# Two mixture-of-experts layers: slots of the fixed experts listed ahead of the ranking, weights queued in order of use, three blocks added by one-hot products

## The chip, the cores and the metric

The kernel is one program on 1 core of one Trainium2 chip. The metric is the device time of one execution in microseconds (us), lower is better. Before the change it was 2995.12 us, the median of 3 runs (2994.06 to 2997.8).

## What is computed

A block of 512 tokens of width 1024 (with 256 context tokens in the first layer) goes through two layers, a mixer and then a mixture of experts each, and after them through a second network (feed-forward, a mixer, feed-forward, a gate). The change is in the mixture of experts, which runs twice: for 768 tokens (layer 0) and for 512 (layer 1).

```python
def hier_moe(h, ...):                      # 4 groups of 8 experts, each 1024 -> 512 -> 1024
    g_idx = argmax(h @ grp_w + grp_b)      # one group for each token
    top_v, top_i = top_k(logits of the 8 experts of that group, 2)
    w = g_prob * softmax(top_v)
    return routed_experts(h, e_idx, w, ...)
# each token's two experts e:  y += w_e * ((silu(x @ w_gate[e]) * (x @ w_up[e])) @ w_down[e])
x = x + g2 * hier_moe(h2)
```

All 32 experts of a layer are computed, and the weights of one are 6.3 MB of float32.

## The kernel before

**Blocks.** `moe` (L830) works by blocks of 128 rows. The experts are ranked by the number of their tokens; experts 0 and 1 are always put first (`FIRST`), so that their weights can be loaded before the routing is known. These two and the next 8 ranked ones (4 in layer 1, `MANY`) have a block each. The rest go in pairs, 64 rows for each of two experts, whose products run side by side in two halves of TensorE's columns. That makes 2 + 8 + 11 = 21 blocks in layer 0 and 2 + 4 + 13 = 19 in layer 1. `turn` (L930) is their order: the two fixed ones, then single and pair in turn, then the pairs that are left. Tokens beyond a block's rows go through a loop that starts at block 12 (`overflow`).

**Routing.** `router` (L601) finds each token's two experts (`oh`), its position among the tokens of that expert (`pos`, L658) and the weights (`v3`). `places` (L664) ranks the experts and gives each choice its block (`ohb`) and its slot. `slots` (L724) turns that into lists by one-hot products: for each block the tokens, the rows and the weights (`stok`, `srow`, `swt`). `order_list` (L700) gives the experts in order of rank, which SyncE reads (L720) to address the weights. `token_major` (L897) writes the normed tokens as rows to DRAM (`h2d`), in 256 KB pieces issued by SyncE (L912).

**Blocks in time.** Block e gathers its rows with an indirect DMA from POOL (L942, tile `xg`), transposes them (L1073), then multiplies by gate, up (L1089) and down (L1108). The down product is scaled (L1115) and scattered to `Yd` in DRAM (L951). Each weight tile is 512 KB; a single block needs 12, a pair 24. They are all issued by SyncE (`raw`, L117, L131), into a ring of 24 tiles: 5 that other stages use too, 13 that exist only here, and 6 that are the split buffers of other stages. A tile's slot is free when the tile 24 places before it has been multiplied. The program's order is gate of block e, down of e-1, up of e.

**End of the stage.** The rows of the last block are not scattered; zeros are written in their place before the first block. After the last down product SyncE reads `Yd` back (L991, 1 MB for each 128 tokens), and the weights of the next stage wait behind these reads. The last block's rows are added to X by products with a one-hot matrix `own` (L1005 to L1012). Then for each 128 tokens the two rows of a token are added on POOL (L1020), transposed (L1030, L1028), scaled and added to X (L1035, L1040, L1041), squared (L1045, L1048), summed over k on VectorE (L1050) and over partitions by a product with ones (L1051). The sums give the norm of the next stage.

Instructions are placed on each engine's queue by a list scheduler with its own model of times, so the order in the trace is not always the order of the text.

Of the kernel before, what the change touches and what calls it, by code (L numbers as in the profile page):

```python
# [21 lines left out]
KD = 8  # L22
# [37 lines left out]
class Kernel:  # L60
    def __init__(self, tc, A):
        self.tc, self.nc, self.A = tc, tc.nc, A
        self.n = 0
        self.live = []
        self.fenced, self.behind, self.last_raw = 0, [], None
# [51 lines left out]
    def raw(self, src, queue=None):  # L117
# [483 lines left out]
    def router(self, l, lt, pool, p2, n_tok):  # L601
# [58 lines left out]
        V.tensor_copy(cnt, pc[:, :NE])  # L660
        self.choice = (oh, pos, v3, cnt)
        return self.places(l, p2, tt)

    def places(self, l, pool, tt):  # L664

        V = self.nc.vector
        oh, pos, _, cnt = self.choice
        mk = lambda name, *s, dt=F32: pool.tile([128, *s], dt, name="p" + name)
# [19 lines left out]
        n = nb + nb % 2  # L688
        ohb = mk("ohb", tt, 2, n)
        V.tensor_tensor(ohb, self.iota[:, :n].unsqueeze(1).unsqueeze(1).to_broadcast([128, tt, 2, n]),  # L690
# [7 lines left out]
        return ohb, slot, nb  # L698
# [25 lines left out]
    def slots(self, pool, rel, rhs, n_tok, name, bufs):  # L724
# [15 lines left out]
        row = pool.tile([128, n], I32, name=name + "row")  # L740
        V.tensor_copy(row, f)
        tok = pool.tile([128, n], I32, name=name + "tok")
        V.tensor_scalar(tok, row, 1, None, op0=ALU.arith_shift_right)
        wt = pool.tile([128, n], F32, name=name + "wt")
# [32 lines left out]
    def overflow(self, l, n_tok, h2d, Yd, p2, x):  # L777
# [7 lines left out]
        with tc.If(nb > 0):  # L785
            with tc.For_i(0, nb, 1) as i:
                with ExitStack() as st:
# [25 lines left out]
                    row, tok, wt = self.slots(pool, rel, rhs, n_tok, "o", 2)  # L813
# [16 lines left out]
    def moe(self, l, n_tok, fg, side_work, stats):  # L830
# [8 lines left out]
        with ExitStack() as st:  # L839
# [4 lines left out]
            with ExitStack() as st1:  # L844
# [3 lines left out]
                with ExitStack() as st2:  # L848
# [65 lines left out]
                    ohb, slot, nb = self.router(l, lt, pool, p2, n_tok)  # L914
                    v3 = self.choice[2]
                    n = ohb.shape[-1]
                    rhs = p2.tile([128, tt, 2, 3 * n], F32R, name="rhs", tag="lg")
                    for c in range(3):
                        V.tensor_tensor(rhs[:, :, :, n * c:n * c + n], ohb,
                                        v3[:, c].bitcast(F32).unsqueeze(3).to_broadcast([128, tt, 2, n]), ALU.mult)  # L920
# [3 lines left out]
                    srow, stok, swt = [pool.tile([128, n], d, name=x) for x, d in (("srow", I32), ("stok", I32), ("swt", F32))]  # L924
                    for a, b in ((srow, row), (stok, tok), (swt, wt)):
                        V.tensor_copy(a, b)
                    self.order_list(l, pool, p2)

                n1 = FIRST[l] + MANY[l]
                turn = list(range(FIRST[l]))  # L930
                for i in range(nb - n1):
                    turn += [FIRST[l] + i] * (i < MANY[l]) + [n1 + i]
                ranks = lambda b: [b] if b < n1 else [2 * b - n1, 2 * b - n1 + 1]
                ysc = []
                with ExitStack() as st2:
                    p2 = st2.enter_context(tc.tile_pool(name=f"moee{l}", bufs=1, reuse_waits="tile"))
                    xg = [xg0] + [p2.tile([128, D], F32, name=f"xg{i}") for i in (1, 2)]
                    ex = []

                    def start(e):  # L940
                        x, b = xg[e % 3], turn[e]
                        nc.gpsimd.indirect_dma_start(  # L942
                            out=x, out_offset=None, in_=h2d,
                            in_offset=bass.IndirectOffsetOnAxis(ap=stok[:, b:b + 1], axis=0),
                            bounds_check=n_tok - 1, oob_is_err=False)
                        ex.append(self.expert(p2, l, [self.ranked_expert(l, r) for r in ranks(b)], x))
                        next(ex[e])

                    def put(e, y):
                        b = turn[e]  # L950
                        ysc.append(nc.gpsimd.indirect_dma_start(  # L951
                            out=Yd, out_offset=bass.IndirectOffsetOnAxis(ap=srow[:, b:b + 1], axis=0),
# [3 lines left out]

                    start(0)
# [3 lines left out]
                    put(nb - 1, xg[2])  # L961
                    for e in range(nb):
# [7 lines left out]
                        if e:  # L970
                            put(e - 1, self.rows_of(p2, next(ex[e - 1]), swt[:, turn[e - 1]:turn[e - 1] + 1]))
# [4 lines left out]
                        if e == self.pause:  # L976
                            self.overflow(l, n_tok, h2d, Yd, p2, xg[(e + 2) % 3])
# [5 lines left out]
                for _ in side_work:  # L983
                    pass
# [1249 lines left out]
```

## Time and profile before

| | |
|---|---|
| median of the timed runs | 2995.12 us (2994.06 to 2997.8) |
| the profiled execution | 2992.93 us, its span 2991.3 us |
| mean granted TensorE clock | 0.97 |
| PE, DVE, ACT, POOL busy | 93%, 41%, 30%, 15% |
| DMA of the span | 643 MB, mean 215 GB/s |

The profile is of one execution; times in it are from the start of its span. PE is TensorE's multiplying, PEld its loading of weights, DVE VectorE, ACT ScalarE, POOL GpSimd, SPq SyncE's queue. A busy PE is not PE at its peak. A number in brackets in a timeline is the idle time ahead of an instruction and what ended it. Layer 0's expert stage runs from about 395 to 931 us, layer 1's from about 1319 to 1838 us.

### The profile page before, as it was taken

How to read it: one execution, taken by the hardware profiler on the slowest of the kernel's cores; microseconds unless marked ns; L12 is line 12 of the kernel's file. 1: busy time of each engine (PE TensorE's matmuls, PEld its weight loads, DVE VectorE, ACT ScalarE, POOL GpSimd, SP SyncE). 2: the span in 40 equal slices, each digit the busy share in tenths (PEclk: the TensorE clock that was granted, in tenths of full speed). 3: DMA queues.
4: the chain of work that ended last, by engine and by line, in shares of the span. 5: the costliest groups of instructions: out<-in, count | busy, mean ns of one | idle time of the engine just before them, and what ended most of it. 6: DMA issues, size and time to landing. Idle time of an engine off the chain costs nothing.

```text
span 2991.3 us, 34947 instructions
## 1 busy us (share of the span) xinstructions
PE 2770.2 (93%) x12662; PEld 1815.0 (61%) x12662; DVE 1231.7 (41%) x2183; ACT 910.5 (30%) x1488; POOL 451.9 (15%) x430
## 2 busy tenths in 40 slices
PE   7989979998997999979999997999999889999998
PEld 3756734433433889844433333778888767888886
DVE  3883431000005566542000004954436777444335
ACT  3563201110102467511110002333225666323223
POOL 1662110000002000010100001371003140000000
PEclk9999989999998999989999998899999999999999
DMA  7558569999997211448999997343333422333331
GB/s 245 198 191 291 177 203 382 403 404 394 399 403 306 77 52 29 149 162 316 406 412 414 412 414 298 92 131 116 94 97 117 134 64 76 97 94 96 99 92 64
DMA packets 211426, 642.98 MB, mean 215 GB/s; under 512 B 32016, under 2 KB 41328, under 8 KB 209968
## 3 DMA queue, kind: packets, MB, share of 16 engines
q1 hardware_dynamic: 195648, 609.38, 56.2%
q0 software_dynamic: 15600, 31.32, 3.0%
q8 instruction: 101, 1.65, 0.2%
q14 instruction: 77, 0.63, 0.1%
HBM read 624.37 MB, written 37.19 MB: 221 GB/s over the span
## 4 chain that ended last, share of the span: by engine, by line
PE 62%; DMA 22%; DVE 9%; issue 4%; ACT 2%; SPq 1%; POOL 0%; DVEq 0%; POOLq 0%; ACTq 0%
PE ps L167 13%; PE ps L168 13%; PE ps L169 13%; PE ps L1089 9%; DMA raw<-exp_w_up 7%; DMA raw<-exp_w_down 6%; DMA raw<-exp_w_gate 6%; PE ps L1108 5%; PE ps L357 3%; DVE wl L90 1%; PE ps L1073 1%; DMA raw<-w_in_ab 1%; PE ps L219 1%; PE ps L1332 0%; DVE X L1035 0%
## 5 line engine op out<-in xcount | busy, mean ns | idle before, releaser
L1089 PE MATMUL ps<-raw,xt 128*64 128x512 f32 (+1 forms) x2048 | 635.6, 602 | 14.9 <-DMA raw<-exp_w_up 10.9
L167 PE MATMUL ps<-Hh,wh 128*128 128x512 f32 (+1 forms) x1320 | 495.5, 381 | 7.2 <-ACT Hh L260 2.1
L169 PE MATMUL ps<-Hh,wl 128*128 128x512 f32 (+1 forms) x1320 | 495.6, 377 | 6.4 <-DVE wl L90 6.3
L168 PE MATMUL ps<-Hl,wh 128*128 128x512 f32 (+1 forms) x1320 | 496.3, 377 | 1.6 <-DVE Hl L267 1.2
L1089 PEld LDWEIGHTS ps<-raw,xt 128*64 128x64 f32 (+1 forms) x2048 | 213.4, 150 | 389.6 <-issue 271.7
L88 ACT ACTIVATE wh<-raw 128x1024 fp32r<-128x1024 f32 (+1 forms) x224 | 231.5, 1039 | 559.8 <-PE ps L168 455.3
L90 DVE TENSOR_TENSOR wl<-raw,wh 128x1024 fp32r<-128x1024 f32 (+1 forms) x224 | 275.4, 1233 | 186.7 <-ACT wh L88 186.0
L1094 DVE TENSOR_TENSOR eh<-ps,eh 128x512 f32<-128x512 f32 x40 | 27.7, 692 | 753.7 <-PE ps L1089 704.8
L1108 PE MATMUL ps<-raw,ht 128*64 128x512 f32 (+1 forms) x1024 | 327.2, 603 | 2.3 <-issue 1.7
L167 PEld LDWEIGHTS ps<-Hh,wh 128*128 128x128 f32 x1320 | 248.9, 190 | 71.2 <-issue 5.6
L168 PEld LDWEIGHTS ps<-Hl,wh 128*128 128x128 f32 x1320 | 249.9, 189 | 52.5 <-issue 2.5
L169 PEld LDWEIGHTS ps<-Hh,wl 128*128 128x128 f32 x1320 | 249.1, 189 | 53.1 <-DVE wl L90 7.6
L1108 PEld LDWEIGHTS ps<-raw,ht 128*64 128x64 f32 (+1 forms) x1024 | 123.2, 150 | 192.7 <-issue 167.3
L1115 ACT ACTIVATE ey<-ps,swt 128x512 f32<-128x512 f32 x76 | 51.4, 686 | 323.8 <-PE ps L1108 305.3
L951 POOL DMA_INDIRECT yd<-ey,srow x38 | 37.9, 997 | 694.5 <-ACT ey L1115 579.5
L408 POOL TENSOR_TENSOR cg<-cg,cp 128x798 f32<-128x798 f32 x60 | 119.1, 1985 | 107.0 <-DVE cv L415 72.1
L1092 ACT ACTIVATE eh<-ps 128x512 f32<-128x512 f32 x40 | 23.9, 597 | 335.0 <-PE ps L1089 335.0
L1078 ACT ACTIVATE xt<-ps 128x512 f32<-128x512 f32 x40 | 23.9, 597 | 279.2 <-PE ps L1089 150.1
L357 PE MATMUL ps<-raw,sc 128*32 128x512 f32 x384 | 97.8, 614 | 3.5 <-DMA raw<-mod_w 3.5
L167 PE MATMUL ps<-Gh,wh 128*128 128x512 f32 x256 | 101.1, 395 | 0.0
L169 PE MATMUL ps<-Gh,wl 128*128 128x512 f32 x256 | 101.0, 395 | 0.0
L168 PE MATMUL ps<-Gl,wh 128*128 128x512 f32 x256 | 101.0, 395 | 0.0
(698 smaller groups left out, 3938.4 us busy)
## 6 DMA issues: line engine op xcount, KB each, us to landing
raw<-exp_w_up SPq DMA_DIRECT2D x256, 512.0 KB
raw<-exp_w_gate SPq DMA_DIRECT2D x256, 512.0 KB
raw<-exp_w_down SPq DMA_DIRECT2D x256, 512.0 KB
raw<-ffn_w SPq DMA_DIRECT2D x132, 512.0 KB
raw<-mod_w SPq DMA_DIRECT2D x96, 512.0 KB
yr<-yd SPq DMA_DIRECT2D x10, 1024.0 KB
X<-xT SPq DMA_DIRECT2D x16, 384.0 KB
raw<-w_in_ab SPq DMA_DIRECT2D x12, 512.0 KB
```

The costliest lines, as they stand in the source:

```text
L88: self.nc.scalar.activation(dst.hi, src, AF.Copy)
L90: self.split_last = eng.tensor_tensor(dst.lo, src, dst.hi.bitcast(F32), ALU.subtract).ins
L167: mm(ps, a.hi, b.hi, start=start, stop=False)
L168: mm(ps, a.hi, b.lo, start=False, stop=False)
L169: mm(ps, a.lo, b.hi, start=False, stop=stop)
L219: self.sums_last = self.nc.tensor.matmul(ps[:, t:t + 1], s, self.ones, start=True, stop=True).ins
L357: nc.tensor.matmul(ps[32 * g:32 * g + 32], self.sc[:, 2 * g + j, 30 - 2 * i:62 - 2 * i], w[:, j * 512:(j + 1) * 512], start=i == 0 and j = ...
L408: nc.gpsimd.tensor_tensor(a, a, t, ALU.add)
L951: ysc.append(nc.gpsimd.indirect_dma_start(out=Yd, out_offset=bass.IndirectOffsetOnAxis(ap=srow[:, b:b + 1], axis=0), in_=y, in_offset=None ...
L1089: mm(ps[s], XT[:, 2 * c + k, s], w[:, 512 * k:512 * k + 512], start=c == 0 and k == 0, stop=c == 3 and k == 1, **kw)
L1108: mm(pss[b][s], HT[:, k, s], w[:, 512 * b:512 * b + 512], start=k == 0, stop=k == 3, **kw)
L1115: self.nc.scalar.activation(y[:, 512 * b:512 * b + 512], pss[b], AF.Copy, scale=wt)
```

## The change

Four edits in `moe` and its helpers.

1. The lists of the two fixed experts are made by a first call of `slots`, from `oh` and `pos` alone, ahead of `token_major` and of `places`; the lists of all other blocks by a second call behind `places`.
2. `turn` has the pair before the single one, and every weight tile of the stage is put on SyncE's queue behind the one that the program asked for before it (`in_turn`).
3. The last three blocks (`owned`), not one, are added to X by one-hot products (`add_own`).
4. The other rows are read back while the last two blocks run (`add_rows`), in 512 KB reads issued by POOL into the ring of weight tiles; the two rows of a token are added on VectorE. Squares and sums are made for each k behind the last block's `add_own`: the sum over partitions by products with ones or squared gains (`gs`), with no sum over k on VectorE but a small one at the end. The next stage's weights no longer wait for the reads.

```diff
@@ raw
-            if ins:
-                st.enter_context(self.tc.issue_after(ins))
+            for i in (ins, self.in_turn and queue is None and self.last_raw):
+                if i:
+                    st.enter_context(self.tc.issue_after(i))
@@ moe
-                    ohb, slot, nb = self.router(l, lt, pool, p2, n_tok)
...
-                    row, tok, wt = self.slots(p2, slot, rhs, n_tok, "s", 2 * tt)
+                    self.router(l, lt, pool, p2, n_tok)
+                    oh, pos, v3, _ = self.choice
...
+                    first = lists("f", oh[:, :, :, :n0], pos, 4)
                     token_major()
                     self.behind = [None] * self.ahead[l] + put_back[1::2]
+                    later = lists("s", *self.places(l, p2, tt), 4)
                     self.order_list(l, pool, p2)
...
-                    turn += [FIRST[l] + i] * (i < MANY[l]) + [n1 + i]
+                    turn += [n1 + i] + [n0 + i] * (i < MANY[l])
...
+                    def add_own(e, pss):
+                        w = swt(turn[e])
+                        YS = self.split_tile(self.turn_of(self.wrings)[0], [128, CH], "w")
...
+                        for k in range(KD):
+                            for i, (o, c) in enumerate(segs):
+                                ps = self.bank("tp")
+                                for j in (YS.hi, YS.lo):
+                                    nc.tensor.matmul(ps[:, :c], j[:, 128 * k:128 * k + 128], own[:, o:o + c], start=j is YS.hi, stop=j is YS.lo)
+                                xs = X[:, k, o:o + c]
+                                V.scalar_tensor_tensor(xs, ps[:, :c], self.mcol(l, 5, k, i), xs, op0=ALU.mult, op1=ALU.add)
+                            yield k
+                    def add_rows():
+                        for t in range(tt):
+                            y = [self.raw(Yv[t][:, j], nc.gpsimd) for j in range(2)]
+                            V.tensor_tensor(y[0], y[0], y[1], ALU.add)
+                            for b in range(2):
...
+                            yield t
+                    own = range(nb - self.owned, nb)
...
-                    put(nb - 1, xg[2])
+                    for e in own:
+                        put(e, xg[2])
...
+                            if e - 1 in own:
+                                for _ in add_own(e - 1, pss):
+                                    pass
+                            else:
+                                put(e - 1, self.rows_of(p2, pss, swt(turn[e - 1])))
                         next(ex[e])
...
+                        if e > own[0]:
+                            for _ in range(-(-tt // (self.owned - 1))):
+                                next(rows, None)
...
-            for t in range(tt):
-                self.rows_read = nc.sync.dma_start(yr[t], Yv[t]).ins
-            self.behind = 12 * [self.rows_read]
...
+                    for k in add_own(nb - 1, pss):
+                        x2 = p2.tile([128, n_tok], F32, name=self.uid("x2"), tag="x2", bufs=2)
+                        a = nc.scalar.activation(x2, X[:, k, :n_tok], AF.Square)
+                        for t in range(tt):
+                            o = m * (KD * t + k)
+                            nc.tensor.matmul(sums[:, o:o + m], x2[:, 128 * t:128 * t + 128], gs[:, k], start=True, stop=True)
+                    self.tail = [a.ins]
```

## Rows read from the trace of the kernel before

**Rows 1.** Page, busy time of each engine, share of the span, instructions.
```profile
PE 2770.2 (93%) x12662; PEld 1815.0 (61%) x12662; DVE 1231.7 (41%) x2183; ACT 910.5 (30%) x1488; POOL 451.9 (15%) x430
```
**Rows 2.** Chain of waits, 900 to 1000 us: start, length, what.
```profile
896.96 10.76 DMA raw<-exp_w_down
907.84 10.93 DMA raw<-exp_w_up
...
935.80 3.83 PE ps L1010 x12
```
**Rows 3.** Windows: stretch, length, busy (count) by engine, clock, DMA share, GB/s.
```profile
456.00:467.00 11.00, 11.00 (x36) 4.15 (x36) 1.85 (x9) 1.37 (x2) 1.00 (x1) 1.00 0.74 236
467.00:478.00 11.00, 11.00 (x52) 4.48 (x49) 1.29 (x2) 1.20 (x2) 1.01 (x1) 1.00 1.01 397
...
800.00:912.00 112.00, 107.36 (x384) 37.27 (x384) 7.33 (x11) 9.68 (x15) 3.33 (x5) 1.00 1.02 403
...
1369.00:1380.00 11.00, 11.00 (x39) 5.08 (x37) 8.19 (x31) 1.10 (x2) 1.02 (x1) 1.00 0.56 201
1380.00:1391.00 11.00, 11.00 (x36) 4.30 (x36) 2.36 (x13) 1.37 (x2) 1.00 (x1) 1.00 0.55 159
...
1700.00:1825.00 125.00, 118.35 (x422) 39.76 (x418) 7.33 (x11) 9.68 (x15) 4.49 (x5) 1.00 1.03 414
```
**Rows 4.** Timeline of the routing in both layers: start, length, instruction.
```profile
378.65 0.55 DVE L658 TENSOR_REDUCE pos<-ox 128x12 f32<-128x384 f32 x1
...
389.45 2.44 DVE L735 TENSOR_SCALAR sB<-iota,pslot 128x128 fp32r<-128x128 f32 x12
...
394.51 1.17 POOL L942 DMA_INDIRECT xg<-h2d,stok  x1 [17.60 <-DVE stok L926]
...
398.86 1.94 PE L1073 MATMUL ps<-ident,xg 128*128 128x128 f32 x8 [6.30 <-DMA xg<-h2d,stok]
...
1305.34 0.42 DVE L658 TENSOR_REDUCE pos<-ox 128x8 f32<-128x256 f32 x1
...
1319.41 1.12 POOL L942 DMA_INDIRECT xg<-h2d,stok  x1 [17.41 <-DMA raw<-exp_w_gate]
```
**Rows 5.** Timeline of SyncE's queue, layer 0.
```profile
344.62 1.28 SPq L131 DMA_DIRECT2D raw<-exp_w_gate  x3
361.82 15.44 SPq L912 DMA_DIRECT2D h2d<-hr  x12
...
418.97 21.00 SPq L131 DMA_DIRECT2D raw<-exp_w_gate  x8
```
**Rows 6.** Timeline of the end of both stages.
```profile
924.26 7.73 PE L1108 MATMUL ps<-raw,ht 128*64 128x512 f32 x32 [0.83 <-issue]
...
931.39 1.32 ACT L998 ACTIVATE ysh<-ps,swt 128x512 fp32r<-128x512 f32 x2 [19.68 <-PE ps L1108]
...
968.79 0.15 DVE L1055 COPY sums<-ps 128x6 f32<-128x6 f32 x1
...
1829.46 8.80 PE L1108 MATMUL ps<-raw,ht 128*64 128x512 f32 x32 [0.83 <-issue]
...
1864.76 2.44 ACT L1048 ACTIVATE x<-X,gcol 128x128 f32<-128x128 f32 x8 [0.92 <-DVE sq L1050]
```
**Rows 7.** Groups by line, 932 to 969 us, then 1838 to 1873 us.
```profile
L1050 DVE TENSOR_REDUCE sq<-x 128x128 f32<-128x1024 f32 x6 | 11.3, 1904 | 1.1 <-ACT x L1045 1.1
L1012 DVE SCALAR_TENSOR_TENSOR X<-ps,mod,X 128x512 f32<-128x512 f32 (+1 forms) x16 | 9.0, 611 | 1.5 <-PE ps L1010 1.4
...
L1035 DVE SCALAR_TENSOR_TENSOR X<-ps,mod,X 128x128 f32<-128x128 f32 x24 | 6.7, 344 | 0.0
...
L1012 DVE SCALAR_TENSOR_TENSOR X<-ps,mod,X 128x512 f32<-128x512 f32 x8 | 5.5, 743 | 0.2 <-PE ps L1010 0.2
```
**Rows 8.** Timeline: prices of the new kinds of work.
```profile
349.41 1.42 PEld L219 LDWEIGHTS ps<-ones,acc 128*128 128x128 f32 x12 [0.41 <-issue]
```
**Rows 9.** Timeline of POOL, the last scatter of layer 0.
```profile
911.99 0.97 POOL L951 DMA_INDIRECT yd<-ey,srow  x1 [31.05 <-DMA raw<-exp_w_up]
```

More of the change, by code (lines that the diff above doesn't have):

```diff
@@ L921, in moe, with lists @@
-                    row, tok, wt = self.slots(p2, slot, rhs, n_tok, "s", 2 * tt)
+                    self.router(l, lt, pool, p2, n_tok)
+                    oh, pos, v3, _ = self.choice
+                    n0, n1 = FIRST[l], FIRST[l] + MANY[l]
+                    nb = n1 + (NE - n1) // 2
+                    def lists(name, one_hot, place, bufs):
+                        n = one_hot.shape[-1]
+                        rhs = p2.tile([128, tt, 2, 3 * n], F32R, name=name + "rhs")
+                        for c in range(3):
+                            V.tensor_tensor(rhs[:, :, :, n * c:n * c + n], one_hot,
+                                            v3[:, c].bitcast(F32).unsqueeze(3).to_broadcast([128, tt, 2, n]), ALU.mult)
+                        return self.slots(pool, p2, place, rhs, n_tok, name, bufs)
@@ L930, in moe @@
-                turn = list(range(FIRST[l]))
+                    srow, stok, swt = [lambda b, x=x, y=y: x[:, b:b + 1] if b < n0 else y[:, b - n0:b - n0 + 1]
+                                       for x, y in zip(first, later)]
+                turn = list(range(n0))
                 for i in range(nb - n1):
-                    turn += [FIRST[l] + i] * (i < MANY[l]) + [n1 + i]
+                    turn += [n1 + i] + [n0 + i] * (i < MANY[l])
                 ranks = lambda b: [b] if b < n1 else [2 * b - n1, 2 * b - n1 + 1]
@@ L957, in moe @@
+                    m = len(stats)
+                    gs = pool.tile([128, KD, m], F32, name="gs")
+                    for i, g in enumerate(stats):
+                        if g is None:
+                            nc.gpsimd.memset(gs[:, :, i], 1.0)
+                        else:
+                            nc.gpsimd.tensor_tensor(gs[:, :, i], g, g, ALU.mult)
+                    own = range(nb - self.owned, nb)
                     start(0)
@@ L1002, in moe @@
-            toks = p2.tile([128, n_tok], F32, name="toks")
-            nc.gpsimd.iota(toks, pattern=[[1, n_tok]], base=0, channel_multiplier=0, allow_small_or_imprecise_dtypes=True)
-            own = p2.tile([128, n_tok], F32R, name="own")
-            V.tensor_scalar(own, toks, tokf, None, op0=ALU.is_equal)
-            for k in range(KD):
-                for i, (o, c) in enumerate(segs):
-                    ps = self.bank()
-                    for j in (YS.hi, YS.lo):
-                        nc.tensor.matmul(ps[:, :c], j[:, 128 * k:128 * k + 128], own[:, o:o + c], start=j is YS.hi, stop=j is YS.lo)
-                    xs = X[:, k, o:o + c]
-                    V.scalar_tensor_tensor(xs, ps[:, :c], self.mcol(l, 5, k, i), xs, op0=ALU.mult, op1=ALU.add)
@@ L1052, in moe @@
-            self.tail = a
-            self.fence()
-            s = self.cst.tile([128, m, tt], F32, name=self.uid("sums"))
-            V.tensor_copy(s, sums[:, :m * tt].rearrange("p (t m) -> p m t", m=m))
+                    for _ in chain(rows, side_work):
+                        pass
+                    sums = self.bank()
+                    for k in add_own(nb - 1, pss):
[4 more added lines that the diff above has]
+                            nc.tensor.matmul(sums[:, o:o + m], x2[:, 128 * t:128 * t + 128], gs[:, k], start=True, stop=True)
@@ L1056, in moe @@
+                    self.tail = [a.ins]
+                    self.in_turn = False
+                    del self.rings[1:]
+                    self.fence()
+                    s = self.cst.tile([128, m, tt], F32, name=self.uid("sums"))
+                    V.tensor_reduce(s, sums[:, :m * tt * KD].rearrange("p (t k m) -> p m t k", m=m, k=KD), axis=AX.X, op=ALU.add)
         return s
+    owned = 3
     def ew(self, name, l, e):
```

119 lines of the change are left out of this document (39 added, 80 removed).

## The prediction

> **What bounds the kernel now.** I read the page first, then the chain of waits, then windows of the two expert stages, then the timelines around their two ends. The page says that PE is busy 93% [rows 1]; in the expert stages that is no bound, because the chain there runs over weight DMAs, eight 512 KB tiles after eight others at 10.8 to 10.9 us [rows 2]. The windows tell the same: from 467 us on the DMA engines are at 1.01 to 1.03 busy and move 397 to 414 GB/s [rows 3]. So from 467 us to the last weight, and in layer 1 from 1391, time is bytes: a tile costs 0.524 MB / 403 GB/s = 1.30 us in layer 0 and 0.524 / 414 = 1.27 us in layer 1. What can be gained there is DMA time that is not used earlier, or bytes. Two places lie outside: the start (nothing to multiply until the first block's rows have come [rows 4]) and the tail behind the last weights (TensorE waits on VectorE [rows 6, 7]).
>
> **Start: lists of the fixed experts.** The first gather goes out at 394.51 us, 15.3 us after `pos` is done at 379.20 (378.65 + 0.55); in layer 1 at 1319.41, 13.65 us after 1305.76 [rows 4]. From `pos` to the one-hot matrices that stands at 389.45, 10.25 us later: this is the ranking, which the new first call doesn't need. In layer 1, whose chain is 13.65/15.3 as long, I take 9.1 us. What the first call keeps is the part from 389.45 to 394.51, 5.1 us, and three small products of `oh` with `v3`. At most 10.2 and 9.1 us are gained, at least nothing: VectorE works its queue in order, and the ranking now stands right behind and may slip between the steps of the new chain, with four buffers of one-hot matrices where there were twelve. I take 6 us for each layer, because the ranking's own steps fill VectorE just as long as before and only some of them can slip in. The gather also waits for the rows in DRAM; SyncE's twelve writes are issued until 377.26 (361.82 + 15.44) [rows 5], 7 us ahead of the new gather, so they are not late yet. This gain is kept to the end: the ring of weights is full before the first block, and no weight can follow until a block has begun to free it.
>
> **Order.** The pair before the single. A single block asks for 12 tiles in the time in which a pair asks for 24. While the first blocks are singles, the ring is full and the DMA engines wait: 236 GB/s at 456 to 467, and 201 and 159 at 1369 to 1391 [rows 3]. These last windows of the slow part are where the third block is now multiplied. With a pair there, they can run full: at most 11 x (1 - 236/403) = 4.6 us in layer 0 and 11 x (2 - 360/414) = 12.4 us in layer 1. At least nothing, if the slots that the ring waits for come free no earlier. I take 4 and 6 us, near the first of the two rows. Putting the tiles strictly in line costs SyncE nothing while it waits on DMA anyway. At the start it does: the first block's last gate tiles are issued at 344.62 only [rows 5], and up to 16 other tiles that went ahead of them must now follow. 20 tiles at 1.30 us are 26 us, and the twelve 256 KB row writes another 12 x 0.65 = 7.8: 344.6 + 33.8 = 378.4, before the new first gather (394.5 - 6 = 388.5). It is hidden by 10 us; without that cover it would eat the head start.
>
> **Rows read beside the weights.** 12 tiles in layer 0 (6 x 128 tokens, two rows each) and 8 in layer 1 now pass while the DMA engines are full: + 12 x 1.30 = 15.6 us and + 8 x 1.27 = 10.1 us for the last weight. The trace has no reads from POOL of this kind beside weights; the bounds are nothing, if the reads fell into gaps, and these bytes, and the windows with a DMA share of 1.02 say bytes. Two scatters fewer and two of zeros more are a wash. The Trainium skill (DMA: Bandwidth & Descriptors, Issuing engines are not separate DMA queues) states that DMAs from any engine run on the same 16 engines and interleave, which speaks against a gain from reading beside. By that rule the reads lengthen the stage by their bytes; if a second queue had room of its own, the sum below would be better by the two terms just named; the share of 1.02 sides with the rule.
>
> **Adding blocks 2 and 3 from the end, and the rows, inside the stage.** Each own block costs VectorE 9.0 us in layer 0 and 5.5 in layer 1 [rows 7] and two steps to split it, some 1.5 us. Each 128 tokens of rows cost it 8 x 0.344 = 2.75 us [rows 7] and an add that I price as two 128x512 steps at 0.743, 1.5 us. All of it: layer 0 2 x 10.5 + 6 x 4.25 = 46.5 us, layer 1 2 x 7 + 4 x 4.25 = 31 us. Cover: scatters of pairs lie 32 us apart (31.05 + 0.97) [rows 9], VectorE is busy 7.33 of 112 us in that stretch [rows 3], and a pair's products need 3 x 7 us of TensorE (32 instructions in 7.1 us, from 924.26 to 931.39 [rows 6]), so about 9 us of each 32 are free there and 29 on VectorE. Two last blocks with their reads take 2 x 31 + 15.6 = 78 us, 46.5 of which VectorE needs. I let 2 us for each layer show. If the cover failed all 77 us would.
>
> **Tail.** Before, layer 0 takes from 931.39 (last down product, when its scaling starts) to 968.79, 37.4 us, and layer 1 from 1838.26 (1829.46 + 8.80) to 1867.20 (the last square), 28.9 us [rows 6]. VectorE fills it: 9.0 + 6.7 + 11.3 us in layer 0 in three groups alone [rows 7]. After: the split (2.1 us: 1.32 on ScalarE [rows 6], then one 0.743 step on VectorE [rows 7]), the one-hot products and X (VectorE 9.0 or 5.5), and the squares on ScalarE beside it. The sum over k goes to TensorE: 48 products in layer 0, each loading a 128x128 tile in two instructions. Twelve such loads took 1.42 us [rows 8], so 96 take 11.4 us, and the 32 one-hot products, 12 of which took 3.83 us at the lower clock [rows 2], take 5.1 at the higher. TensorE, 16.5 us, is then later than VectorE. Layer 0: 2.1 + 16.5 + 1 = 19.6, a gain of 17.8 us. In layer 1 the next stage needs X and the last square first: 2.1 + 5.5 + 0.6 (the square) + 1 = 9.2, a gain of 19.7 us. The next stage's weights find slots when the last blocks are done, 10 to 20 us ahead of their use, so I give them nothing. If TensorE falls to the lower clock in this tail, as it did at 935.8 in the old one [rows 2], layer 0 loses up to 16 us more.
>
> **Sum.** Layer 0: - 6 - 4 + 15.6 + 2 - 17.8 = - 10.2. Layer 1: - 6 - 6 + 10.1 + 2 - 19.7 = - 19.6. Together - 29.8 us against the profiled execution's 2992.93 (its span of 2991.3 and 1.6 around it), so 2963; the median of the runs shown is 2.2 above that execution, so I predict 2965 us.
>
> **Rivals.**
> Head start lost: the strict line on SyncE, or the ranking on VectorE, holds the first block where it was, and the ring starves as before. For it speaks that the hiding is only 10 us; against it, that the line is short of 388. Then starts and order give nothing: - 0.2 in layer 0 and - 7.6 in layer 1, 2987 us.
> Reads for nothing: the ring's waits leave room for the rows, 25.7 us better: 2939 us. Against it, 1.02 in the windows.
> Slower: the last two blocks become VectorE's. TensorE takes its queue in order, so the transposes of rows and one-hot products stand ahead of weight products, three banks must be emptied by VectorE at 0.3 to 0.75 us each, and reads also take 6 of 24 ring slots. Of the 77 us, 4 are in the sum; from 34 us on the change is no gain; at 77 it is 3038. I put it at 3012, two thirds exposed. The page's idle VectorE speaks against it, the in-order queue for it.
>
> **Numbers.** This kernel's runs can't tell less than 0.2% (6 us) from no change, so faster is below 2989 and slower above 3001. Forecast 0.62, head start lost 0.16, reads for nothing 0.07, slower 0.15. Half of the lost head start counts as faster: 0.62 + 0.07 + 0.08 = 0.77; 0.08 same; 0.15 slower. Low end: full start and order gains, no exposure: - 10.2 - 4.6 + 15.6 - 17.8 = - 17 and - 9.1 - 12.4 + 10.1 - 19.7 = - 31, so 2947, and 2942 with part of the cheap reads. High end: the lost head start with 10 us exposed, 2997.
>
> **What would show it.** In the changed profile the first gather should stand near 388 and 1313; windows from the third block on should read about 400 GB/s; the last down weight should land a few us later than before in layer 0 and about the same in layer 1; from the last down product to the norm's sums there should be about 20 us in layer 0, with TensorE behind VectorE, and 9 to the last square in layer 1. It is wrong if row transposes or one-hot products stand on the chain of waits ahead of the last weights, if the DMA share drops below 1 there, or if the first gather doesn't move.

## The result

After the change the kernel takes 3026.1 us (median of 4 runs, 3024.4 to 3031.4), beside 2994.6 before: ratio 1.0107, interval 1.009 to 1.0125. It became 31.5 us slower. The forecast was 2965, with 2997 as its high end.

**Bookkeeping.** From either trace I read, for each layer: S, from the first gate product to the end of the last down product, and T, from there to the instruction that writes the sums of squares. They come from the one run that was profiled; that of after took 3031.4 us, 5.3 above the median.

| us | S0 | T0 | S1 | T1 | span |
|---|---|---|---|---|---|
| before | 531.3 | 36.8 | 513.4 | 33.5 | 2991.3 |
| after | 573.5 | 31.0 | 540.5 | 16.1 | 3029.4 |

The tails became shorter by 23 us together, the stages longer by 69. The start came 3.1 us earlier in layer 0.

The page shows more TensorE work, 62 us over [rows 1], in the same share of the span:

```profile
PE 2832.5 (93%) x12862; PEld 1856.6 (61%) x12862; DVE 1261.1 (42%) x2293; ACT 895.7 (30%) x1438; POOL 443.7 (15%) x445
```

**Start.** Timeline of after, layer 0, the lines that answer to [rows 4]:

```profile
371.62 0.55 DVE L659 TENSOR_REDUCE pos<-ox 128x12 f32<-128x384 f32 x1
...
380.04 1.20 DVE L677 TENSOR_REDUCE prank<-pgt 128x32 f32<-128x1024 f32 x1
...
386.43 0.15 DVE L746 TENSOR_SCALAR ftok<-frow 128x2 int32<-128x2 int32 x1
387.43 1.33 POOL L952 DMA_INDIRECT xg<-h2d,ftok  x1 [10.21 <-DVE pslot L698]
...
397.60 4.73 PE L1100 MATMUL ps<-raw,xt 128*128 128x512 f32 x8
```

The first gather goes out at 387.4, but `pos` is 7 us earlier than before too, and from `pos` (372.17) to the gather it is still 15.3 us: the ranking (`prank`) stands among the steps of the fixed experts' list. Only in layer 1 did that path get shorter (8.4 us instead of 13.65).

**Windows** of after (busy time and count of PE, PEld, DVE, ACT, POOL; granted clock, DMA share, GB/s):

```profile
456.00:467.00 11.00, 11.00 (x27) 4.94 (x26) 2.34 (x13) 1.37 (x2) 1.00 (x1) 1.00 1.03 410
...
1400.00:1411.00 11.00, 11.00 (x44) 4.29 (x43) 9.95 (x41) 0.15 (x1) 1.03 (x1) 1.00 1.02 390
...
880.00:900.00 20.00, 17.13 (x66) 7.86 (x63) 14.04 (x26) 1.37 (x2) 0.00 (x0) 1.00 0.46 154
900.00:940.00 40.00, 36.29 (x129) 12.16 (x128) 12.24 (x32) 1.97 (x3) 3.16 (x6) 1.00 1.03 409
940.00:960.00 20.00, 15.18 (x60) 7.15 (x59) 13.61 (x27) 0.00 (x0) 0.00 (x0) 0.90 0.50 168
```

The first two answer to the slow windows of [rows 3] (236 and 201 GB/s; layer 1 lies 31 us later): the pair ahead of the single filled them, as forecast. New are two holes at the end of layer 0, where the DMA share is 0.46 and 0.50. Against 409 GB/s each lacks 12 us.

**The holes** in SyncE's queue, after, layer 0 (start, length from first issue to last):

```profile
868.43 24.77 SPq L132 DMA_DIRECT2D raw<-exp_w_up  x8
893.71 8.16 SPq L132 DMA_DIRECT2D raw<-exp_w_gate  x8
...
932.62 21.89 SPq L132 DMA_DIRECT2D raw<-exp_w_down  x8
```

Waits of SyncE from 860 to 965 us (total, times, longest):

```profile
SPq L132 <- PE ps L985: 15.9, 2, 15.6
```

L985 is the one-hot product of `add_own`. SyncE holds 15.6 us behind one of them; five of the last block's eight down tiles can't be asked for until then. `add_own` takes its split rows YS (`wh`, `wl`) from the split buffers, and these are also 6 of the ring's 24 slots. In the first hole SyncE's longest wait for TensorE is 6.9 us, for an up product; that YS is behind this hole too is shown only by e1 below.

TensorE's queue in that stretch:

```profile
944.11 0.39 PE L985 MATMUL ps<-own,wh 128*128 128x256 f32 x1
944.33 0.28 PE L985 MATMUL ps<-own,wl 128*128 128x256 f32 x1
...
945.01 1.93 PE L1100 MATMUL ps<-raw,xt 128*64 128x512 f32 x6
...
957.95 3.67 PE L1000 MATMUL ps<-ident,raw 128*128 128x128 f32 x16 [2.94 <-DVE raw L995]
...
963.98 7.14 PE L1119 MATMUL ps<-raw,ht 128*64 128x512 f32 x32 [1.50 <-DVE ht L1112]
```

One-hot products alternate with the last up products until 952, then come the rows' transposes, which wait for VectorE's additions, and only then the last down product: 971.1, where it was 932.0 [rows 6].

**Tail.** After, layer 0, then layer 1:

```profile
971.14 1.26 ACT L975 ACTIVATE wh<-ps,swt 128x512 fp32r<-128x512 f32 x2 [37.23 <-PE ps L1119]
...
975.40 1.48 PE L1058 MATMUL ps<-gs,x 128*128 128x1 f32 x12
...
978.17 2.55 PE L1058 MATMUL ps<-gs,x 128*128 128x1 f32 x12
...
1002.14 0.20 DVE L1064 TENSOR_REDUCE sums<-ps 128x6 f32<-128x48 f32 x1
...
1905.08 0.63 ACT L1055 ACTIVATE x<-X 128x512 f32<-128x512 f32 x1 [1.08 <-PE ps L1058]
...
1908.44 0.23 DVE L1064 TENSOR_REDUCE sums<-ps 128x8 f32<-128x64 f32 x1 [0.53 <-PE ps L1058]
```

The same twelve sum products take 1.48 us, then 2.55 when the granted clock has fallen to the lower level (0.50 over 980 to 1000).

### The profile page after: what moved, and what is told of

The parts are those of the page before. It is cut to its first block, busy times and chain, and to the rows that moved or that the text cites. A ratio compares the mean times of both kernels' runs of the same rounds, so it can differ in the third digit from the quotient of the medians.

```text
span 3029.4 us, 35447 instructions
## 1 busy us (share of the span) xinstructions
PE 2832.5 (93%) x12862; PEld 1856.6 (61%) x12862; DVE 1261.1 (42%) x2293; ACT 895.7 (30%) x1438; POOL 443.7 (15%) x445
## 5 line engine op out<-in xcount | busy, mean ns | idle before, releaser
L1126 ACT ACTIVATE ey<-ps,swt 128x512 f32<-128x512 f32 x60 | 40.0, 686 | 216.6 <-PE ps L1119 214.3
L960 POOL DMA_INDIRECT yd<-ey,srow x30 | 29.9, 996 | 497.0 <-ACT ey L1126 371.9
## 6 DMA issues: line engine op xcount, KB each, us to landing
raw<-yd POOLq DMA_DIRECT2D x20, 512.0 KB, 10.1
```

Of the source, the lines that this page charges most:

```text
L960: ysc.append(nc.gpsimd.indirect_dma_start(out=Yd, out_offset=bass.IndirectOffsetOnAxis(ap=srow(turn[e]), axis=0), in_=y, in_offset=None, b ...
L1126: self.nc.scalar.activation(y[:, 512 * b:512 * b + 512], pss[b], AF.Copy, scale=wt)
```

## Experiments

Ratios are to runs of the kernel before on the same chip, with the interval where there is one. S and T as above. A single run has no interval. e6, e7 and e18 leave out part of the work; each stands for its trace.

| run | us | ratio | S0 | T0 | S1 | T1 |
|---|---|---|---|---|---|---|
| e1_ys_own | 3013.3 | 1.0054 (1.0037 to 1.0071) | 559.4 | 30.1 | 538.4 | 18.2 |
| e2_rows_own | 3031.4 | 1.0109 (1.0092 to 1.0126) | 569.5 | 30.2 | 544.5 | 15.2 |
| e3_both_own | 3045.6 | 1.0158 (1.0141 to 1.0175) | 579.1 | 30.4 | 547.7 | 15.6 |
| e4_start_only | 2991.1 | 0.9982 (0.9972 to 0.9992) | 531.0 | 37.0 | 515.8 | 35.1 |
| e5_rows_early | 3011.2 | 1.0061 (1.0044 to 1.0078) | 564.1 | 28.5 | 534.2 | 15.4 |
| e6_rows_unadded | 2989.2 | one run | 544.8 | 30.8 | 530.5 | 15.4 |
| e7_rows_unread | 2978.3 | one run | 537.4 | 28.3 | 518.5 | 13.9 |
| e8_start_bufs | 2987.7 | 0.9977 (0.9967 to 0.9987) | 530.8 | 38.4 | 517.0 | 35.1 |
| e9_ranking_held | 2982.0 | 0.9952 (0.9938 to 0.9966) | 528.6 | 37.3 | 516.6 | 34.6 |
| e10_no_turn | 2987.0 | 0.9967 (0.9955 to 0.9979) | 529.4 | 38.6 | 516.2 | 34.2 |
| e11_lists_only | 2995.0 | 0.9995 (0.9986 to 1.0004) | 532.1 | 35.6 | 521.3 | 35.1 |
| e12_mix | 2986.4 | 0.9961 (0.9947 to 0.9974) | 529.2 | 37.9 | 528.0 | 15.9 |
| e13_before_shift | 3003.1 | 1.0022 (1.0013 to 1.0031) | 535.1 | 37.4 | 520.9 | 33.7 |
| e14_after_shift | 3021.0 | 1.0082 (1.0067 to 1.0097) | 571.1 | 29.0 | 534.5 | 16.0 |
| e15_held_aligned | 2982.0 | 0.9952 (0.9939 to 0.9966) | 521.4 | 37.7 | 505.0 | 34.1 |
| e16_mix_aligned | 2975.9 | 0.9935 (0.9921 to 0.9948) | 523.7 | 37.5 | 519.8 | 15.0 |
| e17_mix_ring | 2968.6 | 0.9913 (0.99 to 0.9927) | 522.8 | 37.7 | 524.4 | 15.3 |
| e18_sums_left | 2994.7 | one run | 562.1 | 14.1 | 536.4 | 9.7 |

The stretch between the layers (next stage's first product to layer 1's first gate product) differs between 343 and 353 us in kernels with the same start (343.6 in e1, 352.8 in e7), and I did not find why. So terms are taken from S and T, not from single totals. These differ as well between traces of the same work: e13 edits layer 1 alone, and its S0 is 3.8 us above that of before; e18 differs from e1 only behind S0, and its S0 is 2.7 us above. A term of up to 4 us can't be told from nothing.

**e1: YS out of the ring**

```diff
-YS = self.split_tile(self.turn_of(self.wrings)[0], [128, CH], "w")
+YS = Split(*[p2.tile([128, D], F32R, name=self.uid("ys"), tag="ey", bufs=self.eys) for _ in range(2)])
```

> Against the changed kernel only the place of the weighted rows YS differs: they stand in the two row buffers (ey) that the last three blocks leave idle, not in a wh and a wl buffer that are also 6 of the ring's 24 slots. Theory S (slots: a weight tile that takes a wl or wh buffer waits for the one-hot products of the block before): the two holes of layer 0 (154 GB/s over 880 to 900 us, 168 over 940 to 960; each some 12 us at 405 GB/s) fill, the last down product of layer 0 ends 20 to 25 us earlier, that of layer 1 5 to 10 us: 2992 to 3002 us. Theory W (work: TensorE and VectorE have too much to do at the end, with row adds and one-hot products ahead of the last block's): the holes become shorter, but the last down product moves by under 5 us: 3018 to 3027 us. Theory R (the twelve row tiles hold ring slots): no change, holes stay, 3020 to 3030 us.

13 us faster than after. Windows of e1 (the last one is the stretch ahead of the last down product), and its timeline there:

```profile
880.00:900.00 20.00, 20.00 (x71) 7.82 (x71) 11.25 (x19) 1.37 (x2) 0.00 (x0) 1.00 1.03 409
900.00:940.00 40.00, 32.80 (x150) 14.25 (x146) 22.82 (x47) 1.97 (x3) 3.16 (x6) 0.98 0.99 392
940.00:960.00 20.00, 15.84 (x78) 8.23 (x76) 12.66 (x37) 1.94 (x3) 0.55 (x1) 0.96 0.10 35
...
932.50:949.00 16.50, 11.60 (x54) 8.01 (x54) 16.04 (x40) 0.00 (x0) 0.00 (x0) 0.90 0.42 166
```

```profile
941.78 1.87 PE L1000 MATMUL ps<-ident,raw 128*128 128x128 f32 x12
942.81 6.28 DVE L1003 SCALAR_TENSOR_TENSOR X<-ps,mod,X 128x128 f32<-128x128 f32 x24
...
949.74 7.09 PE L1119 MATMUL ps<-raw,ht 128*64 128x512 f32 x32 [1.92 <-DVE ht L1112]
```

The holes are gone, S0 is 14.1 us shorter, S1 only 2.1. Theory S holds for a third of what layer 0's stage lost. The last weight lands at 938.6, and the last down product ends 18 us later: one-hot products and row transposes stand in front of it, held by VectorE's additions into X. From 932.5 to 949 VectorE is busy 16.04 of 16.5 us, TensorE 11.60. That is theory W, for the rest.

**e2 and e3: rows out of the ring**, in three tiles of their own; e3 has e1's edit too.

```diff
-y = [self.raw(Yv[t][:, j], nc.gpsimd) for j in range(2)]
+y = [p2.tile([128, D], F32, name=self.uid("yr"), tag="yr", bufs=3) for j in range(2)]
+for j in range(2):
+    nc.gpsimd.dma_start(y[j], Yv[t][:, j])
```

> The rows read back stand in three tiles of their own, not in the weights' ring; YS stays in the ring. Theory R: the holes at the end of layer 0 fill, 2995 to 3008 us. Theory S: both holes stay (SyncE waits some 15 us for one-hot products), 3020 to 3035 us; three tiles instead of twelve make the last reads later, which may add some 5 us. Theory W: no change, 3020 to 3030 us.

> YS in the row buffers and the rows in three tiles of their own: nothing but weights in the ring. Theory S: as e1 within 6 us. Theory R: as e2. Theory W: 3015 to 3027 us whatever stands where. If S and R both hold a part, this is the fastest of the three, near 2985 us.

Windows of e2:

```profile
880.00:890.00 10.00, 9.33 (x34) 4.23 (x33) 6.87 (x12) 1.38 (x2) 0.00 (x0) 1.00 0.18 45
...
930.00:940.00 10.00, 9.31 (x35) 4.30 (x35) 7.24 (x12) 1.38 (x2) 0.53 (x1) 1.00 0.25 85
```

e2's holes stay and its time is what theory S had, so theory R (the rows' slots) falls as their cause. But with three tiles each pair of reads waits for the additions before it, 8.5 us apart in e3, and e3 was slower than any theory allowed. It says nothing on S and R together.

**e4: start and order alone**, the tail as before the change.

> Only the start of the change: the fixed experts' lists ahead, the pair first, weights strictly in order of use; the tail is that of the kernel before. Prediction's step: first gathers some 6 us earlier and a fuller queue in both layers, about 20 us off 2994.6 (2972 to 2980 us). As the trace of the changed kernel reads (first gate product 3.1 us earlier in layer 0, 4.3 in layer 1): 2985 to 2990 us. Rival: a strict order costs more than the earlier start brings, over 2996 us.

5 us, where 22 had been counted. The first gate product is 3.3 us earlier in layer 0 and S0 the same, so that head start is kept. In layer 1 it is 2.2 us earlier by itself, and S1 loses 2.4; both are less than two traces differ by.

**e5 to e7: rows one block earlier; rows read but not added; not read.** All three on e1.

```diff
# e5
-if e > own[0]:
+if e >= own[0]:
# e6
-V.tensor_tensor(y[0], y[0], y[1], ALU.add)
-...                       # transposes and additions to X
+for i in y:
+    V.tensor_copy(i[:, :1], i[:, 1:2])
# e7: no raw(), nothing of the two
```

> e1 (3013.3 us) with the rows read back and added one block earlier: three tiles at each of blocks 18 and 19 of layer 0, two at 16 and 17 of layer 1, none beside the last block. Theory W (what is left after the slots is work in front of the last block's down products: in e1 the row transposes and their additions run from 941.8 to 947.7 us between the last up and the last down products): the last down product ends 5 to 10 us earlier in layer 0 and 3 to 6 in layer 1, 2998 to 3006 us. Theory B (the read-back's bytes alone, 12 tiles at 1.30 us and 8 at 1.27, set what is left): 3010 to 3015 us. Rival: the row tiles now hold ring slots earlier and open a new hole: over 3016 us.

> e1 with the rows read back into the ring but neither turned nor added (left out: the additions of all blocks but the last three; one small copy per row tile stays, so that it is read). Theory W: the last down product of layer 0 ends within 3 us of 397.5 + 531.3 + 15.6 = 944 us (e1: 956.8), and the whole is 2990 to 3000 us. Theory B: 3010 to 3014 us.

> e6 without the read-back itself (left out: reading and adding the rows of all blocks but the last three). If bytes on a full queue cost their time: 15.6 us less than e6 in layer 0 and 10.1 in layer 1, 2965 to 2974 us. If the reads go beside the weights for nothing: as e6 within 5 us.

Last down product of e5, e6 and e7, a window of e5, then SyncE's last weights of the stage in e6 and in e7, and a window of e7:

```profile
954.62 7.14 PE L1119 MATMUL ps<-raw,ht 128*64 128x512 f32 x32 [0.79 <-DVE ht L1112]
```
```profile
935.94 7.14 PE L1111 MATMUL ps<-raw,ht 128*64 128x512 f32 x32 [0.96 <-DVE raw L996]
```
```profile
928.96 7.14 PE L1109 MATMUL ps<-raw,ht 128*64 128x512 f32 x32 [0.78 <-DVE ht L1102]
```
```profile
850.00:880.00 30.00, 16.34 (x64) 6.93 (x61) 8.66 (x21) 0.60 (x1) 6.40 (x12) 0.80 1.03 408
```
```profile
913.00 16.31 SPq L132 DMA_DIRECT2D raw<-exp_w_down  x8
```
```profile
904.76 9.31 SPq L132 DMA_DIRECT2D raw<-exp_w_down  x8
```
```profile
900.00:936.00 36.00, 34.87 (x138) 12.77 (x134) 12.38 (x20) 1.97 (x3) 0.00 (x0) 1.00 0.76 289
```

e6 ends the last down product at 943.1 (944 expected): the additions cost 14.6 us of S0 and 7.9 of S1. The reads cost 7.4 and 12.0. In layer 0 they hold the weights up for longer than that: the last tile is asked for at 929.3 in e6 and at 914.1 in e7, 15.2 us earlier, and lands at 939.1 and 923.7. But e7's last down product ends 12.4 us behind its last weight, e6's 4.0 behind: without the reads the end of the stage is TensorE's, busy 34.87 of the 36 us up to there. What e7 keeps, two more blocks by one-hot products, lengthens S0 by 6.4 against e4 and S1 by 2.7. e5 was a miss: the additions are gone from in front of the last down product, yet S0 is 4.7 us longer than in e1. Now the rows' reads stand ahead of weights (TensorE is busy 16 of 30 us while DMA is full), and the one-hot products that are left fill TensorE to 952. Its 3011.2 us lie in theory B's range, but bytes are not the reason: the last weight lands at 938.4 and the last down product ends at 961.8. The granted clock was 0.80 in the window shown and 0.92 over 880 to 933, so a part of the loss is the lower clock; how much is not shown. That TensorE's time is short in the last blocks wherever the rows stand is argued from this. In layer 1 the earlier rows gave 4.2 us.

**e8 to e11: the start.** e8: twelve (eight) one-hot buffers instead of four. e9: e8, and the ranking behind the list. e10: e8 without the strict order. e11: e10 with the single block first.

```diff
# e8
-first = lists("f", oh[:, :, :, :n0], pos, 4)
+first = lists("f", oh[:, :, :, :n0], pos, 2 * tt)
# e9: self.listed is the list's last instruction on VectorE
-V.tensor_copy(cnt, self.pc[:, :NE])
+with self.tc.issue_after(self.listed):
+    V.tensor_copy(cnt, self.pc[:, :NE])
# e10
-self.in_turn = True
# e11, beside that
-turn += [n1 + i] + [n0 + i] * (i < MANY[l])
+turn += [n0 + i] * (i < MANY[l]) + [n1 + i]
```

> The start edits alone (e4: 2991.1 us) with as many one-hot buffers for the fixed experts' list as it has steps (12 and 8 instead of 4), so that no step waits for TensorE and the ranking's operations on VectorE don't slip between them. Theory: from the last position to the first gather 10 to 12 us instead of 15.3, the first gate product of each layer 3 to 5 us earlier and half of it kept at the end: 2984 to 2989 us. Rival: the gather's landing (7.7 us beside weight tiles) takes it back: 2989 to 2993 us.

> e8 (2987.7 us) with the ranking's first operation on VectorE put behind the last of the fixed experts' list, so that it cannot slip in. Theory (start is VectorE's order): from the last position to the first gather 11 us or less instead of 15.3 (15.4 in e8), first gate product 3 to 4 us earlier in each layer, kept in layer 0 and not in layer 1: 2983 to 2986 us. Rival: the gather then meets more weight tiles on the DMA engines and lands as late as before: 2986 to 2990 us.

> e8 without the strict order of the weight tiles on SyncE (lists, pair first and buffers stay). Theory (the strict order costs rate in layer 1, where 1500 to 1700 us moved 412 GB/s before and 405 in e4 and e8): 412 to 415 GB/s there again, layer 1 some 8 us shorter, 2979 to 2983 us. Rival (the rate has another reason): 405 there, 2985 to 2991 us.

> e8 without the strict order and with the single block ahead of the pair, as before the change: of the start only the early lists are left. Prediction's step (pair first fills the queue early: 4 us in layer 0, 6 in layer 1): some 10 us slower than e10, near 2990. Rival: the blocks' order moves nothing at the end, within 3 us of e10.

Timeline of e9:

```profile
382.79 1.55 POOL L953 DMA_INDIRECT xg<-h2d,ftok  x1 [3.09 <-DVE pkey L675]
...
387.81 1.94 PE L1086 MATMUL ps<-ident,xg 128*128 128x128 f32 x8 [6.75 <-DMA xg<-h2d,ftok]
...
392.07 2.64 DVE L739 TENSOR_SCALAR sB<-iota,pslot 128x128 fp32r<-128x128 f32 x12
...
395.05 5.22 PE L1102 MATMUL ps<-raw,xt 128*128 128x512 f32 x8
```

e8 did not do what it was built for: the gather still came 15.4 us after `pos`, the first gate product 1.2 us earlier than in e4, and the intervals of the two overlap. In e9 the gather comes 8.8 us after `pos`, and its rows are transposed at 388; the product still starts only at 395, because the other blocks' lists (`sB`) now stand on VectorE and TensorE ahead of it. In total e9 is 0.25% better than e8, at the edge of the intervals. Pair first is worth 0.28% (e10 against e11), 8 us; the lists alone nothing that can be told, but e11 has the lower rate of layer 1 in it, which e13 below prices; the strict order nothing good: e8 and e10 overlap. That rate did not come back in e10 or e11, so the strict order is not its reason: 405 to 406 GB/s over 1450 to 1800 us in all variants, 413 before.

**e12: the changed tail in layer 1 alone**, with e5's edits, on e8.

> e8's start in both layers, layer 0 with the tail of the kernel before, layer 1 with the changed tail as in e5 (YS in the row buffers, rows one block earlier). From the traces: up to the next stage's first product in layer 0 as e4 (972.7), from there to the sums of layer 1 894.4 as e5 instead of 897.5: 2984 to 2986 us. If the tail of layer 1 costs more than it gives, as in layer 0: over 2990 us.

2986.4, against 2987.7 of e8: in layer 1 S1 + T1 is 543.9 instead of 552.1, but the stretch between the layers took 7 us more. By their intervals the two can't be told apart.

**e13 and e14: the address of the ring.** In the built programs layer 1's thirteen extra ring buffers start at byte 81408 = 159 x 512 of each partition before, and at 81568 after: the lists kept in `pool` moved them by 160 bytes.

```diff
 xg0 = pool.tile([128, D], F32, name="xg0")
+if (0, 8)[l]:                        # e13, on before; e14, on after: (0, 88)
+    pool.tile([128, (0, 8)[l]], F32, name="pad")
```

> The kernel before, with an unused tile of 32 bytes per partition ahead of layer 1's thirteen ring buffers: they start at 81440 instead of 81408 = 159 x 512 bytes, nothing else differs. Theory A (address: tiles whose buffers start at a multiple of 512 bytes land faster; the change moved layer 1's buffers off one, to 81568): layer 1 falls from 413 GB/s over 1450 to 1800 us to 405, about 9 us longer, 3002 to 3007 us. Theory O (the rate has to do with the order or the lists): no change, 413 GB/s, 2992 to 2998 us.

> The changed kernel, with an unused tile of 352 bytes per partition ahead of layer 1's thirteen ring buffers, so that they start at 81920 = 160 x 512 bytes. Theory A: 412 to 415 GB/s over 1450 to 1800 us (405 in the changed kernel), 7 to 10 us off 3026: 3016 to 3020 us. Theory O: no change, 3023 to 3029 us.

Windows of before, e13, after and e14:

```profile
1450.00:1800.00 350.00, 331.66 (x1234) 121.68 (x1233) 25.25 (x38) 31.25 (x49) 21.13 (x21) 0.99 1.03 413
```
```profile
1450.00:1800.00 350.00, 331.35 (x1203) 121.23 (x1201) 23.86 (x36) 31.66 (x50) 21.15 (x21) 0.99 1.02 406
```
```profile
1450.00:1800.00 350.00, 330.65 (x1211) 126.36 (x1212) 25.83 (x39) 32.25 (x51) 22.58 (x23) 1.00 1.02 405
```
```profile
1450.00:1800.00 350.00, 331.54 (x1227) 126.02 (x1226) 25.84 (x39) 32.25 (x51) 24.41 (x26) 0.99 1.02 411
```

32 bytes made the kernel before 0.22% slower (6.9 us), with 413 GB/s turned to 406; putting the buffers back on a multiple of 512 gave the changed kernel 5 us by the medians, 0.25% by the ratios (the intervals overlap; the rate went from 405 to 411 GB/s and S1 fell by 6.0 us). Theory A holds, theory O falls. This part of the loss is no property of the four edits.

**e15 to e17: what the addresses are worth.** e15: e9 with all 24 buffers on multiples of 512. e16: the same for e12 with e9's edit. e17: as e16, but only the thirteen extra buffers of each layer moved (`pad` of 32 and 88 elements, 128 and 352 bytes), the other eleven left in place.

> e9 (2982.0 us) with all 24 ring buffers of both layers starting at multiples of 512 bytes (one small constant moved behind the rings, unused tiles of 32, 96 and 384 bytes). Theory A, if the gain goes with the share of buffers (13 of 24 gave 2% in layer 1 before): 418 to 422 GB/s in both layers, some 18 us off each stage of 500 us, if TensorE follows: 2945 to 2960 us. If TensorE, busy 95% there, is the next bound: 2960 to 2972. Theory O: 2980 to 2986.

> e12 (2986.4 us: tail of the change in layer 1 only, early rows, YS in the row buffers) with e9's held ranking and all ring buffers at multiples of 512 bytes. Theory A: as e15, with 3 us less from the tail of layer 1 as e12 had against e8 (1 us in the medians), unless the faster weights leave TensorE behind with the one-hot products and row transposes: then 3 to 10 us more than e15.

> As e16, but only the thirteen extra ring buffers of each layer start at multiples of 512 bytes; the five and six others stand where they stood, because with these moved the stages behind layer 1 took 14 us longer in e15 and e16 (1133 us from the sums of layer 1 to the end, 1118 in e9). Theory: 412 to 414 GB/s over 1450 to 1800 us, 402 to 405 over 500 to 850, the stages behind at 1118 us again: 2966 to 2973 us. If the eleven other buffers gave most of e16's rate: 2975 to 2980 us. If the stages behind are slow for another reason: 2978 us or more.

e15 moves 405 GB/s in layer 0 (400 in e9) and 415 in layer 1 (406); 418 to 422 in both had been expected, and a gain of 10 us or more. Its stages are 7.2 and 11.6 us shorter than e9's, and yet the total is the same: from the sums of layer 1 to the end it takes 1133 us where e9 takes 1118. There TensorE's products read the split buffers that were moved. Groups by line in the feed-forward stage, of e9, then e15:

```profile
L169 PE MATMUL ps<-Hl,wh 128*128 128x512 f32 x224 | 87.1, 389 | 0.0
```
```profile
L169 PE MATMUL ps<-Hl,wh 128*128 128x512 f32 x225 | 89.0, 396 | 0.0
```

389 ns became 396; the lengths of all 2592 such products (`Hh` and `Hl` by `wh`, `Hh` by `wl`) behind layer 1 add up to 15.8 us more in e15, which is the loss. e15 moved these buffers by 224 bytes and what lies behind them by 32; which of the two does it was not separated. e17 moves neither: 1119 us behind layer 1 again, 404 GB/s in layer 0 (400 before), 410 in layer 1 (412 to 414 expected, 414 in e16), and 2968.6 us, 0.87% faster than before and by its median the fastest of all. It holds the early lists, pair first and the strict order, e9's order on VectorE, the old tail in layer 0, the new one in layer 1, and aligned buffers.

**e18: the tail without most sums**, on e1.

```diff
-for t in range(tt):
+for t in range(tt if k == KD - 1 else 0):
```

> e1 (YS in the row buffers) with the sums of squares of the last of eight groups of rows only (left out: the sums of the other seven, 84 of 96 loads in layer 0). In e1 the tail of layer 0, from the last down product to the sums, takes 30.1 us at the lower clock with TensorE busy throughout. If TensorE sets the tail (12 loads take 2.6 us there): 30.1 - 7 x 2.6 = 12 to 15 us, bounded below by VectorE's 8 x 1.23 + 3. If VectorE and ScalarE set it: 24 us or more.

Windows of layer 0's tail in e1, then e18:

```profile
956.00:986.00 30.00, 29.32 (x132) 26.37 (x128) 13.25 (x21) 10.96 (x13) 4.87 (x9) 0.60 0.26 90
```
```profile
962.00:976.00 14.00, 10.29 (x46) 6.61 (x44) 12.00 (x20) 10.29 (x12) 4.87 (x9) 0.92 0.53 189
```

T0 falls from 30.1 to 14.1 us, and the clock stays at the higher level until about 974, 2 us from its end. The sum products on TensorE set this tail. What the lower clock alone costs can't be separated from them by this run: both go together.

## Why the prediction was wrong

The steps of the forecast against the traces, us, by S and T (own blocks e7 less e4, reads e6 less e7, additions e1 less e6, slots after less e1, tail after less e4):

| step | forecast L0, L1 | measured L0, L1 |
|---|---|---|
| reads beside the weights | 15.6, 10.1 | 7.4, 12.0 |
| adding in the stage | 2, 2 | 35.1, 12.7 |
| - own blocks | | 6.4, 2.7 |
| - rows' additions | | 14.6, 7.9 |
| - ring slots held by YS | | 14.1, 2.1 |
| tail | -17.8, -19.7 | -6.0, -19.0 |

With the -5.5 us of the start the measured steps add up to 36.7 us, beside 31.5 by the medians and 38.1 by the two profiled runs.

**The step that failed** is "Adding blocks 2 and 3 from the end, and the rows, inside the stage": 4 us in the sum, 48 on the chip. It failed in two ways.

First, it priced the added work on VectorE and found room there. The total was about right: 46.5 us forecast, and VectorE is busy 46.7 us from 880 to 960 in e1. But it does not spread over the 78 us that were counted as cover: a good part comes behind the last up products, where VectorE has no room left (16.04 of 16.5 us). The forecast also put TensorE's room at about 9 of 32 us per pair, but never set TensorE's share of the new work against it. That share, from the traces: the one-hot products of a block take about 8 us (in e5, 933 to 953 us: 2 x 0.85 + 6 x 0.97 + 0.51), the transposes of three row tiles 3.5 (48 for six tiles in 7.0 us in e1), and TensorE stood idle ahead of the two kinds for VectorE for 6.6 us in e1. That is some 15 us for each of two blocks, and the second block's part comes when hardly a weight is left to hide it. With the own blocks alone (e7) the end of the stage is TensorE's; the 14.6 us of the rows' additions are work of both engines in turn, and e6 leaves out both parts, so no run shows which of them sets it. The windows had TensorE at 107.36 of 112 us [rows 3]; I read that as no bound because the chain ran over DMAs.

Second, the diff says `split_tile(self.turn_of(self.wrings)[0], ...)`, and the kernel's description says that the split buffers are six of the ring's slots. I had the rows hold ring slots, as part of a rival, and did not see that YS does. e1 shows its price, and e2 that the rows' slots were not it.

**The tail of layer 0** is the second miss. 19.6 us were forecast with TensorE behind VectorE at the higher clock; TensorE did set it (e18), at the lower one, and it took 31.0. The forecast named that loss (up to 16 us) and left it out of the sum. Layer 1 came near the forecast: 13.3 us from the last down product to the last square instead of 9, and T1 17.4 us shorter. One reading was off by 0.6 us, with no weight in the sum: the 32 down products of [rows 6] took 7.73 us, not 7.1; the scaling starts before the last of them has ended.

**Start and order.** -22 us forecast, -5.5 measured (e4). The signs that I named appeared (gather at 387.4 and, less the shift, 1313.5; full windows from the third block), and pair first gave its 8 of 10 us (e10, e11). Of the rest, 6.9 us went to the addresses (e13), which nothing in the trace of before could have shown, and part to the ranking that slipped in (e9). The sign "gather near 388" was a poor one: it stood there for another reason, since `pos` itself was earlier.

**Reads.** 19.4 us by S, 25.7 forecast. The Trainium skill (DMA: Bandwidth & Descriptors, Issuing engines are not separate DMA queues) states that DMAs of all engines share the same 16; e6 against e7 agrees: the last weight lands 15.4 us later in layer 0 and 12.2 in layer 1 (15.6 and 10.1 forecast). The step was right. That the stage of layer 0 became only 7.4 us longer by it is because TensorE was the later one there without the reads (e7).

**The rivals.** "Slower" was the case, given 0.15 and 3012 us: its in-order queue is what happened, with TensorE short of room first (e7) and VectorE too once the rows came (e1). Its price, 51 of 77 us exposed, is close to the 47.8 measured by luck in part: 16.2 of these are YS's slots, which it did not name. What I named as proof of error came true as well: the DMA share fell to 0.46 and 0.50 at the end, and row transposes stood ahead of the last down product.

## What to carry to other kernels

Work moved into a stage that transfers bound has to be set against every engine's room there, TensorE's in-order queue first: 15 us of it for a block do not fit into a room of 9, and when the work comes counts as much as how much it is. A buffer borrowed from a ring delays the ring by the time it is held, so each new tile is to be traced to its pool before its edit is costed at nothing. And when a rate changes in a stage that an edit doesn't touch, compare the buffers' addresses before looking for a reason in the order of work.

## What the runs showed of the hardware

- Thirteen of 24 weight buffers moved by 32 bytes off a multiple of 512: 413 GB/s became 406, with the DMA engines busy throughout. The Trainium skill (DMA: Bandwidth & Descriptors, How a descriptor splits into AXI transactions) says for reads that a descriptor that doesn't start on a 256-byte boundary fetches from the boundary below and pays the extra beats. The buffers here are where the transfers write, which the page doesn't speak of. If its rule held there, 32 bytes on a packet of 3.6 KB would be about 1%, for 13 of 24 tiles 0.5% (an estimate from that page and the mean packet of SyncE's queue in that window); the run shows 1.7%. In e9 layer 0's thirteen buffers stood on a multiple of 128, not of 256, and moved at 400 GB/s; on multiples of 512 (e17) it was 404. Which boundary counts was not tried.
- With the split weights on multiples of 512 (and other tiles moved by 32 bytes) TensorE's 128x512 products took 396 ns instead of 389 (e15): a layout that was good for the DMA was bad for TensorE. Which of the two moves does it was not separated.
- TensorE, busy 29.3 of 30 us in the tail of e1, was granted 0.60 on the mean (1.00 up to about 962 us, 0.50 from there, the lower of its two levels); what it did before the clock fell, and while it stayed low, were products with one column behind 128x128 loads beside the one-hot products.
